# Two blocks behind each of three layer norms in fp32 from (x - shift) g, and lo of the expert tiles to VectorE at tile 41

## The chip, the cores and the metric

One core of one Trainium2 chip. The metric is device microseconds (us) of one execution; a kernel's time is the median of its runs. TensorE (PE) multiplies, VectorE (DVE) and ScalarE (ACT) work on tiles and read TensorE's results from PSUM, GpSimd (POOL) works on tiles in SBUF and issues gathers, and SyncE (SP) holds the queue that issues the other transfers.

## The reference

A two-layer encoder on 256 tokens (272 with 16 meta tokens in front), 1024 features. Layer 0 mixes tokens with a gated recurrence, layer 1 with a gated convolution of 31 taps; each is followed by a retrieval from 128 x 128 = 16384 experts, and behind each of the four sub-layers stands a layer norm:

```python
def layer_norm(x, g, b):
    mu = mean(x); var = mean(square(x - mu))
    return (x - mu) * rsqrt(var + LN_EPS) * g + b

def peer_block(xc, w_query, sub_keys, expert_u, expert_v):
    q = (xc @ w_query).reshape(c, HEADS, 2, HALF)
    scores = einsum('chpk,pnk->chpn', q, sub_keys)
    s1, i1 = top_k(scores[:, :, 0], 16)
    s2, i2 = top_k(scores[:, :, 1], 16)
    s, flat = top_k(s1[..., :, None] + s2[..., None, :], 16)
    g = softmax(s)
    act = gelu(expert_u[expert] . xc)
    return sum(g * act * expert_v[expert])

for i in range(2):
    h = layer_norm(ALPHA * h + mixer(h), ln_mix[i])
    h = layer_norm(ALPHA * h + peer(h), ln_ffn[i])
```

So a matrix product stands behind each of the first three norms: `w_query` of layer 0, `pw1` of the convolution, `w_query` of layer 1.

## The kernel before

Activations are kept with features on the 128 partitions, in eight blocks of 128 (NB), and tokens along the row (272 in layer 0, 256 in layer 1). A weight matrix is walked in output blocks of 128 columns, 512 KB each, loaded by SP into one of four raw buffers (`load`, L122 to L128).

Most products run in three parts of reduced fp32 (`linears`, L166): ScalarE rounds a raw block to `hi` (L137), the remainder `lo` is made by VectorE or GpSimd (L144), and TensorE makes 8 products each of `hi` by x's `hi`, `hi` by x's `lo`, and `lo` by x's `hi` (L172), in that order. `lo` has two buffers, so the `lo` of a block can be made one block ahead. The first two blocks (`defer=2`) are interleaved. `linears_whole` (L203, L208) instead multiplies a block in plain fp32, with 8 products; `w_in` and `pw1` go that way.

**The norms** (`normed`, L273). While the last blocks of the linear ahead of the norm come out, each finished block has the mean of all features, guessed from three blocks, taken away (`shift`), its square is made by ScalarE (`square`, L745) and summed by TensorE into `var`. Behind the last block TensorE sums the mean of what is left (`mu`) and the last square (L287), ScalarE squares the mean (L289), TensorE takes it from `var` (L290), and 13 products of ones follow whose result isn't used (`keep_clock`, L292). VectorE then subtracts `mu` from the eight blocks (L280), makes the reciprocal root with a Newton step (L310 to L312) and multiplies the eight blocks by it (L316). ScalarE and GpSimd apply gain and bias. Behind the first and the third norm (`norm_split`, L320) this gives x's `hi` at once (L324, L326), and VectorE makes x's `lo` (L331, L332). The query blocks' copies to q are VectorE's (L516).

**The convolution stage** (`conv_glu`, L1033). Blocks of `pw1` come in pairs, gate and value: ScalarE makes the sigmoid of the gate (L1045), VectorE multiplies (`hp`, L1051). ScalarE makes the first two taps of a block (L1074, L1076), VectorE the other 29 (L1078), for five blocks and most of a sixth; the rest goes through TensorE with diagonal matrices, which ScalarE makes (L1014).

**The expert stage** (`peer`, L496). Tokens are scored, and VectorE finds the top 16 of each head, in two token tiles of up to 128 (`topk_steps`, L777): 16 searches of the keys' scores, 8 of the sums, then copies of the indices and a one-hot product that reads the chosen indices out (L818, L821, L826). Meanwhile TensorE walks the 128 expert tiles U: 64 in the loop of L556, whose results `u_store` (L537) takes. There `lo` is made by GpSimd up to tile 45 and by VectorE from tile 46 (LO_FROM). Sixteen tokens are handled apart with gathered rows: from tile 40 (DOTS_FROM), at every second tile, GpSimd issues a gather (`few_rows`, L893) and, two steps later, VectorE makes a dot product (`few_dot`, L900), ten in all. From tile 54 the softmax of each token tile (L830) and the transposes of the chosen indices (`topk_out`, L959) follow. Behind tile 64 the one-hot weights of the experts are made (L577).

Instructions are ordered on each engine by a scheduler when the kernel is built; the order on an engine is then fixed. `issue_after(i)` puts what it holds behind i on i's engine. `pins` ties the rounding of the next weights to points of the norm.

Of the kernel before, what the change touches and what calls it, by code (L numbers as in the profile page):

```python
# [17 lines left out]
P = 128  # L18
# [17 lines left out]
DOTS_FROM, DOTS, AHEAD, LO_FROM = 40, 10, 2, 46  # L36
# [23 lines left out]
class Trunk:  # L60
    def __init__(self, tc, a):
        self.tc, self.nc, self.a = tc, tc.nc, a
        self.early = []
        self.squares = []
        self.last_diag = None
        self.turn = {}
        self.pins = []
        self.ahead = {}

# [140 lines left out]

    def split_x(self, src, hi, lo, hi_on="a"):
# [61 lines left out]
    def normed(self, sp, y, n, shifted=False):  # L273
# [8 lines left out]
        if shifted:  # L282
# [7 lines left out]
            self.mm = nc.tensor.matmul(var[:, :n], self.minus, sq[:, :n], start=False, stop=True)  # L290
            i, self.early_hi = self.early_hi, None
            self.keep_clock(13)  # L292
# [19 lines left out]
        nc.vector.scalar_tensor_tensor(r[1], r[1], 1.5, r[0], op0=OP.add, op1=OP.mult)  # L312
        for k in range(NB):
# [22 lines left out]
    def recurrent(self):  # L336
        tc, nc, a = self.tc, self.nc, self.a
        n = T0
        with tc.tile_pool(name="mix0", bufs=2) as sp:
# [7 lines left out]
            gw = sp.tile([P, 4, NB, P], F32, name="gw", bufs=1)  # L347
# [101 lines left out]

            self.linears([a["w_out"][b] for b in range(NB)], lambda k, lo: (hl if lo else hh)[:, k, :], n,  # L450
# [32 lines left out]
    def to_peer(self, sp, y, layer, n):  # L483
# [4 lines left out]
        def done(k):  # L488
            if k % 4 == 3:
# [3 lines left out]
                        lambda k: xs(k, 0)[:, :n], lambda k: xs(k, 1)[:, :n], done, True)  # L493
        return xs

    def peer(self, layer, n, xs):  # L496
# [10 lines left out]
        with tc.tile_pool(name=f"few{layer}", bufs=1) as kp:  # L507
# [5 lines left out]
            with tc.tile_pool(name=f"top{layer}", bufs=1) as sp:  # L513
                q = sp.tile([P, 2 * HEADS, nq], F32, name="q")
                self.linears([a["w_query"][layer, b] for b in range(2 * HEADS)], xs, nq, FULL,
                             lambda b, ps: nc.vector.tensor_copy(q[:, b, :], ps), defer=2,  # L516
# [3 lines left out]
                for c0, m in ctiles:  # L520
# [8 lines left out]
                    picked.append((c0, m, *self.topk(sp, sc, m)))  # L529
# [215 lines left out]
    def square(self, sp, y, i, n):  # L745
# [3 lines left out]
        sq = self.nc.scalar.activation(to, y[:, i, :n], AF.Square)  # L749
        if i == NB - 2:  # L750
# [26 lines left out]
    def topk_steps(self, sp, sc, m, H):  # L777
# [19 lines left out]
        for h in range(H):  # L797
# [19 lines left out]
        pairs = [m, 2 * H * K, K // 2, 2]  # L817
        nc.vector.tensor_tensor(oh[:m].rearrange("p g k (a b) -> p (g k) a b", b=2),  # L818
                                self.iota16[:m].rearrange("p (a b) -> p a b", b=2)[:, None].to_broadcast(pairs),
                                pf[:m, :, None, :].to_broadcast(pairs), op=OP.is_equal)  # L820
        nc.vector.tensor_tensor(oh[:m], oh[:m],  # L821
# [376 lines left out]
```

## Time and profile before

| | us |
|---|---|
| median of 3 runs | 1840.94 (1838.32 to 1842.51) |
| the profiled execution's own time | 1839.31 |
| its span | 1837.5 |
| TensorE busy | 1789.9 (97%) |
| VectorE busy | 1530.3 (83%) |
| ScalarE busy | 906.9 (49%) |
| GpSimd busy | 480.7 (26%) |

In the profile a time such as 117.33 is us from the start of the span. TensorE's busy time counts products from issue to modelled end, so it includes what they wait inside the engine. A plain fp32 product stands as two records. In a timeline a row gives start, length, engine, line, operation and shapes, how many were merged, and in brackets the idle time ahead of it with what ended it. The three norms of the change end near 117, 924 and 1053; the expert loops of 64 tiles begin near 181 and 1114. Each stage has its own limit, so a share of the whole span says little of any of them.

### The profile page before, as it was taken

The numbers are of one execution on the slowest core, as the hardware profiler recorded it, in microseconds if no ns is written. First come the engines' busy times: TensorE is split into PE (matmuls) and PEld (weight loads), VectorE is DVE, ScalarE is ACT, GpSimd is POOL, SyncE is SP. The second block draws the span as 40 slices with busy tenths as digits, with TensorE's granted clock in tenths as the row PEclk, the third lists the DMA queues.
The fourth block names the chain that finished last, engine by engine and source line by source line (L and its number), as shares of the span: only waits on it lengthen the run. The fifth ranks groups of instructions, "written<-read, shape, count | busy, mean of one in ns | idle before, by whom it ended". The sixth has DMA issues, their size and how long they took to land.

```text
span 1837.5 us, 35134 instructions
## 1 busy us (share of the span) xinstructions
PE 1789.9 (97%) x13599; PEld 1696.7 (92%) x13599; DVE 1530.3 (83%) x2812; ACT 906.9 (49%) x1478; POOL 480.7 (26%) x328
## 2 busy tenths in 40 slices
PE   8999998999999999999999999999999999999997
PEld 7889998999999999999878799999999999999996
DVE  7776997889998787777689859997889988868876
ACT  6544544554444544885432545445544444545542
POOL 1112998100001231222000017992000012423310
PEclk9999999999999999999999999999999999999998
DMA  5444566755557887988532365668555568989883
GB/s 196 138 164 159 169 193 220 244 182 165 162 168 250 308 318 268 321 276 279 176 115 79 106 192 157 191 195 286 180 167 171 164 237 316 333 298 336 294 279 127
DMA packets 110231, 394.10 MB, mean 214 GB/s; under 512 B 12144, under 2 KB 13296, under 8 KB 109936
## 3 DMA queue, kind: packets, MB, share of 16 engines
q1 hardware_dynamic: 91632, 324.74, 53.3%
q0 software_dynamic: 18432, 67.12, 10.5%
q8 instruction: 107, 1.75, 0.4%
q14 instruction: 60, 0.49, 0.1%
HBM read 386.50 MB, written 5.31 MB: 213 GB/s over the span
## 4 chain that ended last, share of the span: by engine, by line
PE 84%; DVE 10%; POOL 2%; issue 2%; ACT 1%; DMA 1%; POOLq 0%; SPq 0%; DVEq 0%; ACTq 0%
PE u L172 41%; PE acc L636 22%; PE acc L640 12%; PE u L208 3%; DVE cy L1078 2%; POOL lo L144 2%; DVE odd L1078 2%; DVE lo L144 1%; PE g L594 1%; PE g L595 1%; PE sps L526 1%; PE wide_ps L869 1%; DMA raw<-peer_v 1%; PE var L759 0%; DVE x L280 0%
## 5 line engine op out<-in xcount | busy, mean ns | idle before, releaser
L137 ACT ACTIVATE hi<-raw 128x1024 fp32r<-128x1024 f32 x560 | 592.5, 1059 | 637.2 <-PE u L172 227.2
L144 DVE TENSOR_TENSOR lo<-raw,hi 128x1024 fp32r<-128x1024 f32 x468 | 572.1, 1227 | 179.8 <-PE acc L640 65.8
L172 PE MATMUL u<-xs,hi 128*128 128x240 f32 (+3 forms) x4608 | 580.7, 278 | 3.6 <-ACT xs L326 3.5
L172 PEld LDWEIGHTS u<-xs,hi 128*128 128x128 f32 x4608 | 548.9, 191 | 5.1 <-ACT xs L326 4.5
L636 PE MATMUL acc<-w,hi 128*128 128x480 f32 (+1 forms) x1984 | 458.3, 373 | 1.9 <-DVE w L217 1.9
L636 PEld LDWEIGHTS acc<-w,hi 128*128 128x128 f32 x1984 | 354.4, 188 | 35.1 <-DVE w L217 2.3
L172 PE MATMUL u<-xs,lo 128*128 128x240 f32 (+3 forms) x2304 | 314.7, 277 | 12.7 <-POOL lo L144 11.8
L172 PEld LDWEIGHTS u<-xs,lo 128*128 128x128 f32 x2304 | 286.9, 191 | 15.0 <-POOL lo L144 13.3
L640 PEld LDWEIGHTS acc<-w,lo 128*128 128x128 f32 x2048 | 268.0, 190 | 15.0 <-DVE lo L144 4.3
L640 PE MATMUL acc<-w,lo 128*128 128x240 f32 (+1 forms) x2048 | 271.9, 274 | 2.4 <-DVE lo L144 2.3
L144 POOL TENSOR_TENSOR lo<-raw,hi 128x1024 fp32r<-128x1024 f32 x92 | 240.0, 2625 | 84.3 <-ACT hi L137 64.7
L895 POOL DMA_INDIRECT rows<-u_rows,ids x64 | 94.0, 1469 | 641.0 <-DVE sv L786 450.0
L895 POOL DMA_INDIRECT rows<-peer_v,ids x64 | 102.1, 1595 | 227.3 <-DVE few_out L930 118.3
L208 PE MATMUL u<-x,raw 128*128 128x272 f32 x512 | 121.1, 397 | 7.0 <-DMA x<-h 5.2
L208 PEld LDWEIGHTS u<-x,raw 128*128 128x128 f32 x512 | 98.1, 192 | 28.0 <-DMA raw<-w_in 5.2
L904 DVE SCALAR_TENSOR_TENSOR rows<-rows,wide 128x1024 f32<-128x1024 f32 x64 | 79.0, 1234 | 0.3 <-DMA rows<-u_rows,ids 0.3
L601 ACT ACTIVATE act_b<-g 128x368 f32<-128x368 f32 (+43 forms) x58 | 22.6, 390 | 113.4 <-DVE act_b L564 95.2
L930 DVE SCALAR_TENSOR_TENSOR few_out<-rows,act,few_out 128x1024 f32<-128x1024 f32 x60 | 76.7, 1279 | 1.2 <-DMA rows<-peer_v,ids 1.2
L577 DVE TENSOR_TENSOR AB<-iota,iT 128x2048 f16<-128x2048 f16 x58 | 70.5, 1219 | 0.1
L594 PE MATMUL g<-AB 128*128 128x128 f16 x464 | 58.6, 220 | 0.0
L595 PE MATMUL g<-Bl,AB 128*128 128x128 f16 x464 | 58.0, 219 | 0.0
L217 DVE TENSOR_TENSOR w<-act_b,w 128x960 fp32r<-128x960 f32 (+1 forms) x32 | 35.9, 1122 | 22.7 <-ACT w L214 22.7
(255 smaller groups left out, 1710.1 us busy)
## 6 DMA issues: line engine op xcount, KB each, us to landing
raw<-peer_u SPq DMA_DIRECT2D x256, 512.0 KB
raw<-peer_v SPq DMA_DIRECT2D x248, 512.0 KB
raw<-w_query SPq DMA_DIRECT2D x32, 512.0 KB
raw<-pw SPq DMA_DIRECT2D x24, 512.0 KB
raw<-w_in SPq DMA_DIRECT2D x16, 512.0 KB
raw<-w_out SPq DMA_DIRECT2D x8, 512.0 KB
wide<-wide SPq DMA_DIRECT2D x8, 512.0 KB
raw<-peer_v SPq DMA_DIRECT2D x16, 256.0 KB
```

The source lines that it names most:

```text
L137: self.act_hi = nc.scalar.activation(hi, raw, AF.Copy).ins
L144: i = e.tensor_tensor(lo[:, s], raw[:, s], hi[:, s].bitcast(F32), op=OP.subtract)
L172: self.mm = nc.tensor.matmul(ps[:, :n], l[:, k, :], xs(k, r)[:, :n], start=start, stop=stop)
L208: self.mm = self.nc.tensor.matmul(ps[:, :n], raw[:, k, :], x[:, k, :n], start=k == 0, stop=k == NB - 1)
L594: nc.tensor.matmul(ps[:, c, :], A, Bh, start=True, stop=False)
L595: nc.tensor.matmul(ps[:, c, :], A, Bl, start=False, stop=True)
L636: self.mm = nc.tensor.matmul(acc[b][:, :2 * n].rearrange("p (a t) -> p a t", a=2), hi, w[:, :, :n], start=j == 0, stop=j == NK - JG - 1, s ...
L640: self.mm = nc.tensor.matmul(main[b][:, :n], hi if p_ else lo, w[:, i, :n], start=False, stop=j == NK - 1 and not p_, skip_group_check=True)
L895: self.nc.gpsimd.indirect_dma_start(out=t, out_offset=None, in_=table, in_offset=bass.IndirectOffsetOnAxis(ap=few["ids"][:, i, k:k + 1], a ...
L904: self.nc.vector.scalar_tensor_tensor(t, t, 1.0, few["x"], op0=OP.mult, op1=OP.mult, accum_out=few["act"][:, i:i + 1])
L930: nc.vector.scalar_tensor_tensor(few["out"], t, w, few["out"], op0=OP.mult, op1=OP.add)
L1078: nc.vector.scalar_tensor_tensor(z, h, w, z, op0=OP.mult, op1=OP.add)
```

## The change

At each of the three norms the first two blocks of the product behind it are no longer made from the normed x. With d = x - shift, the normed row is ((d - mu) rstd) g + b, so a product with weights W is rstd (W(d g) - mu W g) + W b. ScalarE writes d g for each block as its square is made (`square`), two more columns hold -g and b (`pre_open`), and TensorE multiplies both weight blocks by these in plain fp32 (`pre_products`), in place of the 13 products of ones. The product that completes the variance stands behind the second of the eight pairs. ScalarE copies `mu` out of PSUM (`still`). `pre_take` then adds mu times the column of -g, multiplies by rstd, and hands over the column of b as the bias. The two weight blocks are loaded when `pre_open` stands in the program: ahead of `w_out`, ahead of the sums that collect layer 0's experts, and ahead of `pw2`.

In the expert loop, `lo` comes from VectorE from tile 41; the gathers and dots start at tile 48 and go at three of four tiles; the top-k of the second token tile is written out up to its 24 searches, and its other steps, with the one-hot work in two halves, follow one per tile from tile 41, each behind that tile's `lo`. The start of each softmax also stands behind the tile's `lo`.

```diff
-DOTS_FROM, DOTS, AHEAD, LO_FROM = 40, 10, 2, 46
+DOTS_FROM, DOTS, AHEAD, LO_FROM = 48, 10, 2, 41
...
+    def pre_open(self, sp, n, gain, bias, i, srcs, ws=None):
+        t = sp.tile([P, NB, T0 + 2], F32, tag="pre_x", name="pre_x", bufs=1)[:, :, :n + 2]
+        if ws is None:
+            ws = sp.tile([P, 2, NB, P], F32, tag="pre_w", name="pre_w", bufs=1)
+        for w, src in zip((ws[:, 0], ws[:, 1]), srcs):
+            self.nc.sync.dma_start(w.rearrange("p k n -> p (k n)"), src)
+        o = _OFF[gain] + i
+        self.nc.gpsimd.tensor_scalar(t[:, :, n], self.par[:, o:o + NB], -1.0, None, op0=OP.mult)
+        self.nc.gpsimd.tensor_copy(t[:, :, n + 1], self.par[:, _OFF[bias] + i:_OFF[bias] + i + NB])
+        self.pre = t, o, ws
+
+    def pre_products(self, sp, mu, spread):
+        t, _, ws = self.pre
+        n = t.shape[2]
+        units = [(self.bank(3 + i, "pre"), w) for i, w in enumerate((ws[:, 0], ws[:, 1]))]
+        for k in range(NB):
+            for ps, raw in units:
+                i = self.nc.tensor.matmul(ps[:, :n], raw[:, k, :], t[:, k, :], start=k == 0, stop=k == NB - 1)
+            if k == 1:
+                with self.tc.issue_after(i.ins):
+                    spread()
+        n -= 2
+        still = sp.tile([P, T0], F32, tag="still", name="still", bufs=1)[:, :n]
+        self.nc.scalar.activation(still, mu[:, :n], AF.Copy)
+        self.pre, self.pre_out = None, (still, n, [ps for ps, _ in units])
+
+    def pre_take(self, i, add=None):
+        nc = self.nc
+        mu, n, units = self.pre_out
+        ps = units[i]
+        cols = self.cp.tile([P, 2], F32, tag=f"pre_c{i}", name="pre_c", bufs=1)
+        nc.vector.tensor_copy(cols, ps[:, n:n + 2])
+        t = ps[:, :n]
+        nc.vector.scalar_tensor_tensor(t, mu, cols[:, 0:1], t, op0=OP.mult, op1=OP.add)
+        nc.vector.tensor_tensor(t, t, self.rstd, op=OP.mult)
+        if add is not None:
+            nc.vector.tensor_tensor(cols[:, 1:2], cols[:, 1:2], add, op=OP.add)
+        return t, cols[:, 1:2]
...
-            self.mm = nc.tensor.matmul(var[:, :n], self.minus, sq[:, :n], start=False, stop=True)
+            self.pre_products(sp, mu, lambda: nc.tensor.matmul(var[:, :n], self.minus, sq[:, :n], start=False, stop=True))
             i, self.early_hi = self.early_hi, None
-            self.keep_clock(13)
...
+            self.pre_open(sp, n, "ln_mix_g", "ln_mix_b", 0, a["w_query"][0, 0:2], pre_w)
             self.linears([a["w_out"][b] for b in range(NB)], lambda k, lo: (hl if lo else hh)[:, k, :], n,
...
+        self.pre_q = [self.pre_take(i) for i in range(2)]
         return xs
...
-                self.linears([a["w_query"][layer, b] for b in range(2 * HEADS)], xs, nq, FULL,
-                             lambda b, ps: nc.vector.tensor_copy(q[:, b, :], ps), defer=2,
+                for b, (t, bias) in enumerate(self.pre_q):
+                    nc.scalar.activation(q[:, b, :], t, AF.Identity, bias=bias)
+                self.linears([a["w_query"][layer, b] for b in range(2, 2 * HEADS)], xs, nq, FULL,
+                             lambda b, ps: nc.vector.tensor_copy(q[:, 2 + b, :], ps), defer=2,
...
-                    picked.append((c0, m, *self.topk(sp, sc, m)))
+                    if c0 + m < n:
+                        picked.append((c0, m, *self.topk(sp, sc, m)))
+                    else:
+                        slow = self.topk_steps(sp, sc, m, HEADS, 2)
+                        for _ in range(3 * HEADS):
+                            next(slow)
+                        picked.append((c0, m))
...
-                    k, odd = divmod(j - DOTS_FROM, 2)
-                    if early and 0 <= k < DOTS + AHEAD and not odd:
+                    if j >= LO_FROM and len(picked[-1]) == 2:
+                        with tc.issue_after(self.dve_lo.ins):
+                            try:
+                                next(slow)
+                            except StopIteration as end:
+                                picked[-1] += end.value
+                    k, step = divmod(3 * (j - DOTS_FROM), 4)
+                    if early and 0 <= k < DOTS + AHEAD and step < 3:
...
-                        with tc.issue_after(last.ins):
+                        with tc.issue_after(last.ins), tc.issue_after(self.dve_lo.ins):
                             picked[t] = c0, m, idx, self.softmax(sp, fv, m)
...
+        t, o, _ = self.pre
+        self.nc.scalar.activation(t[:, i, :n], y[:, i, :n], AF.Copy, scale=self.par[:, o + i:o + i + 1])
...
+        w = 2 * H // parts
+        for g in range(0, 2 * H, w):
...
+                                    pf[:m, g * K:(g + w) * K, None, :].to_broadcast(pairs), op=OP.is_equal)
+            yield
...
+            self.pre_open(sp, n, "ln_ffn_g", "ln_ffn_b", 0, (a["pw1"][NB], a["pw1"][0]))
             self.collect(sp, acc, x, n)
...
+            self.pre_open(sp, m, "ln_mix_g", "ln_mix_b", NB, a["w_query"][1, 0:2])
...
+        for i in range(2):
+            consume(i, *self.pre_take(i, self.col("conf_b_pw1", NB * (1 - i))))
+        self.linears_whole([a["pw1"][b + o] for b in range(1, NB) for o in (NB, 0)], x, n,
+                           lambda i, ps: consume(i + 2, ps), (0, 1, 2, 7, 6))
...
-            z2 = sp.tile([P, m], F32, tag="odd", name="odd", bufs=6)
+            z2 = sp.tile([P, m], F32, tag="odd", name="odd", bufs=4)
```

## Rows read from the trace of the kernel before

**Rows 1.** The chain of waits that ended last, by engine (page, part 4).

```profile
PE 84%; DVE 10%; POOL 2%; issue 2%; ACT 1%; DMA 1%; POOLq 0%; SPq 0%; DVEq 0%; ACTq 0%
```

**Rows 2.** Waits of TensorE: who waited for whom: us in total, times, longest.

```profile
PE u L172 <- POOL lo L144: 11.8, 8, 3.6
```

**Rows 3.** Timeline behind the first norm: start us, us, engine, line, operation, [idle before].

```profile
112.53 2.97 PE L226 MATMUL idle<-ones 128*128 128x512 f16 x13
...
117.33 0.40 PE L172 MATMUL u<-xs,hi 128*128 128x272 f32 x1 [1.83 <-ACT xs L326]
...
124.58 1.21 DVE L144 TENSOR_TENSOR lo<-raw,hi 128x1024 fp32r<-128x1024 f32 x1
...
126.98 1.16 PE L172 MATMUL u<-xs,lo 128*128 128x272 f32 x8
...
129.97 1.16 PE L172 MATMUL u<-xs,lo 128*128 128x272 f32 x8
```

**Rows 4.** Timeline behind the second norm, into the convolution stage.

```profile
918.77 0.40 ACT L289 ACTIVATE sq<-mu 128x272 f32<-128x272 f32 x1
...
919.20 2.87 DVE L280 TENSOR_TENSOR x<-x,mu 128x272 f32<-128x272 f32 x8 [0.96 <-ACT sq L289]
...
924.56 17.70 PE L208 MATMUL u<-x,raw 128*128 128x272 f32 x76 [1.75 <-ACT x L984]
...
927.35 1.28 ACT L1045 ACT_TABLE_LOAD   x1
...
929.00 0.49 ACT L1045 ACTIVATE sg<-u,par 128x272 f32<-128x272 f32 x1 [0.37 <-PE u L208]
...
929.39 1.85 ACT L1014 ACTIVATE diag<-ident,par 128x128 f32<-128x128 f32 x6
...
932.29 0.50 DVE L1051 SCALAR_TENSOR_TENSOR hp<-u,par,sg 128x272 f32<-128x272 f32 x1 [5.76 <-PE u L208]
```

**Rows 5.** Busy time by stretch: PE, PEld, DVE, ACT, POOL, PEclk, DMA share, GB/s.

```profile
940.00:960.00 20.00, 20.00 (x89) 16.56 (x88) 20.00 (x52) 4.46 (x9) 0.00 (x0) 1.00 0.44 143
```

**Rows 6.** Timeline behind the third norm.

```profile
1060.52 1.22 DVE L144 TENSOR_TENSOR lo<-raw,hi 128x1024 fp32r<-128x1024 f32 x1
...
1062.16 1.10 PE L172 MATMUL u<-xs,lo 128*128 128x256 f32 x8
```

**Rows 7.** Timeline of TensorE, layer 0: expert tiles 40, 46 and 47 begin.

```profile
291.07 1.96 PE L172 MATMUL u<-xs,hi 128*128 128x240 f32 x16
...
315.92 1.96 PE L172 MATMUL u<-xs,hi 128*128 128x240 f32 x16
...
318.61 1.95 PE L172 MATMUL u<-xs,hi 128*128 128x240 f32 x16
```

**Rows 8.** Timeline of TensorE, layer 1: expert tiles 40 and 46 begin.

```profile
1223.34 1.95 PE L172 MATMUL u<-xs,hi 128*128 128x224 f32 x16
...
1244.76 1.95 PE L172 MATMUL u<-xs,hi 128*128 128x224 f32 x16
```

**Rows 9.** Timeline of GpSimd, layer 0, tiles 41 to 43.

```profile
292.50 7.89 POOL L144 TENSOR_TENSOR lo<-raw,hi 128x1024 fp32r<-128x1024 f32 x2
...
300.54 4.05 POOL L895 DMA_INDIRECT rows<-u_rows,ids  x1
```

**Rows 10.** Timeline of VectorE, layer 0: last top-k search, sum of the one-hot step.

```profile
285.85 0.42 DVE L805 FIND_INDEX8 fi<-fv,r 112x8 uint32<-112x256 f32 x1
...
298.21 4.42 DVE L826 TENSOR_REDUCE idx<-oh 112x256 f32<-112x4096 f16 x1
```

**Rows 11.** Timeline, layer 0, tiles 54 to 64: VectorE, and a wait of TensorE.

```profile
336.15 1.22 DVE L904 SCALAR_TENSOR_TENSOR rows<-rows,wide 128x1024 f32<-128x1024 f32 x1
...
345.17 2.35 DVE L144 TENSOR_TENSOR lo<-raw,hi 128x1024 fp32r<-128x1024 f32 x2
...
351.28 2.35 DVE L144 TENSOR_TENSOR lo<-raw,hi 128x1024 fp32r<-128x1024 f32 x2
...
364.75 1.17 PE L172 MATMUL u<-xs,lo 128*128 128x240 f32 x8 [0.44 <-DVE lo L144]
```

More of the change, by code (lines that the diff above doesn't have):

```diff
@@ L68, in __init__ @@
         self.ahead = {}
+        self.pre = None
     def col(self, name, i):
@@ L312, in normed @@
         nc.vector.scalar_tensor_tensor(r[1], r[1], 1.5, r[0], op0=OP.add, op1=OP.mult)
+        self.rstd = r[1]
         for k in range(NB):
@@ L346, in recurrent @@
             self.early.append(self.load(a["w_in"][2]))
-            gw = sp.tile([P, 4, NB, P], F32, name="gw", bufs=1)
+            gw, pre_w = (sp.tile([P, 4, NB, P], F32, tag="gw", name="gw", bufs=1) for _ in range(2))
             lam = self.par[:, _OFF["lru_lambda"]:_OFF["lru_lambda"] + 2 * NB]
@@ L775, in topk, with topk_steps @@
                 return done.value
-    def topk_steps(self, sp, sc, m, H):
+    def topk_steps(self, sp, sc, m, H, parts=1):
         nc = self.nc
@@ L816, in topk_steps @@
         oh = sp.tile([P, 2 * H, K, K], F16, tag="cand", name="oh", bufs=1)
[L817 to L821, printed above, removed]
-                                s16[:m].rearrange("p a h k -> p (a h) k")[:, :, None, :].to_broadcast([m, 2 * H, K, K]),
-                                op=OP.mult)
-        yield
-        idx = sp.tile([P, 2, H, K], F32, tag=f"idx{H}", name="idx", bufs=2)
-        nc.vector.tensor_reduce(idx[:m].rearrange("p a h k -> p (a h) k"), oh[:m], op=OP.add, axis=AX.X)
-        yield
+        idx = sp.tile([P, 2, H, K], F32, tag=f"idx{H}", name="idx", bufs=2)
+        w = 2 * H // parts
+        pairs = [m, w * K, K // 2, 2]
+        for g in range(0, 2 * H, w):
+            nc.vector.tensor_tensor(oh[:m, g:g + w].rearrange("p g k (a b) -> p (g k) a b", b=2),
+                                    self.iota16[:m].rearrange("p (a b) -> p a b", b=2)[:, None].to_broadcast(pairs),
+                                    pf[:m, g * K:(g + w) * K, None, :].to_broadcast(pairs), op=OP.is_equal)
+            yield
+        for g in range(0, 2 * H, w):
+            s = s16[:m].rearrange("p a h k -> p (a h) k")[:, g:g + w, None, :]
+            nc.vector.tensor_tensor(oh[:m, g:g + w], oh[:m, g:g + w], s.to_broadcast([m, w, K, K]), op=OP.mult)
+            yield
+        for g in range(0, 2 * H, w):
+            nc.vector.tensor_reduce(idx[:m].rearrange("p a h k -> p (a h) k")[:, g:g + w], oh[:m, g:g + w],
+                                    op=OP.add, axis=AX.X)
+            yield
         return idx, fv
@@ L1039, in conv_glu, with consume @@
         state = {}
-        def consume(i, ps):
+        def consume(i, ps, bias=None):
             b = i // 2
@@ L1044, in consume @@
                 sg = sp.tile([P, n], F32, tag="sg", name="sg")
-                g = nc.scalar.activation(sg, ps, AF.Sigmoid, bias=self.col("conf_b_pw1", NB + b))
+                g = nc.scalar.activation(sg, ps, AF.Sigmoid, bias=self.col("conf_b_pw1", NB + b) if bias is None else bias)
                 state.setdefault("first", g)
@@ L1050, in consume @@
                 nc.gpsimd.memset(hp[:, n:n + HALO], 0.0)
-                nc.vector.scalar_tensor_tensor(hp[:, 0:n], ps, self.col("conf_b_pw1", b), state["sg"],
+                nc.vector.scalar_tensor_tensor(hp[:, 0:n], ps, self.col("conf_b_pw1", b) if bias is None else bias, state["sg"],
                                                op0=OP.add, op1=OP.mult)
@@ L1056, in consume @@
                     self.split_x(hp, *parts[b])
-        self.linears_whole([a["pw1"][b + o] for b in range(NB) for o in (NB, 0)], x, n, consume, (0, 1, 2, 7, 6))
+        for i in range(2):
+            consume(i, *self.pre_take(i, self.col("conf_b_pw1", NB * (1 - i))))
+        self.linears_whole([a["pw1"][b + o] for b in range(1, NB) for o in (NB, 0)], x, n,
+                           lambda i, ps: consume(i + 2, ps), (0, 1, 2, 7, 6))
         s = META - HALO
```

## The prediction

> **What bounds the kernel now.** I read the chain of waits first. TensorE holds 84% of it and VectorE 10% [rows 1], so the change is worth what it takes out of TensorE's queue, except in a stage where VectorE sets the end. Next the waits of TensorE: in the query and expert products it waited for a `lo` made on GpSimd eight times, 11.8 us in all, 3.6 us the longest [rows 2]. Then the timeline around the three norms. Behind the first, 13 idle products begin at 112.53 and the first query product comes only at 117.33 [rows 3]: a hole of 4.8 us, filled with work that computes nothing. The other two norms look alike. Behind the second lies the convolution, where VectorE is busy 20.00 of 20.00 us [rows 5], so that stage ends when VectorE ends, and what counts is when its first tap can start. Last, the expert stage: tile 40 of layer 0 begins at 291.07 and tile 46, the first whose `lo` is on VectorE, at 315.92, where six tiles at 2.69 would be 16.1 [rows 7]. GpSimd is the reason: two of its `lo` took 7.89 us and the gather behind them 4.05 [rows 9].
>
> **The norms: the products.** A block of eight fp32 products runs in 16 records, and 76 records took 17.70 us [rows 4], 0.23 each. So two blocks are 32 x 0.23 = 7.4 us, plus 0.5 for the variance product put between. They start where the idle products and the one ahead of them started, about 112.1 behind the first norm, and end at 120.0, 2.6 us after the old first query product [rows 3]. The variance itself stands behind four of the 16 products, 8 x 0.23 = 1.8 us late; I cost that at nothing, because the eight subtractions of the mean (2.87 us [rows 4]) cover it. Without that cover it is 1.8 us on the path in each norm.
>
> **The norms: what comes ahead of the subtractions.** The change adds two ScalarE operations at the end of each sum: (x - shift) g of the last block, ahead of the square of the mean, and the copy of the mean, behind it. That square took 0.40 us, and behind the second norm the subtractions start at 919.20, where it ends [rows 4], though they use nothing of it: both read the mean's bank. The copy reads that bank too, so I let the subtractions wait for both, 2 x 0.40 = 0.8 us a norm, between 0 (the scheduler puts the copy behind them) and 1.2. The Trainium skill's page "PSUM — Partial Sum Buffer", section "PSUM bank collisions raise a hardware error", says that two engines on one bank are kept apart, reads against reads too. By that rule the 0.8 us are due in full; by none of it they would be 0.4, for the copy of the last block alone; row 919.20 agrees with the rule.
>
> **First norm.** Two query blocks fewer are 2 x 2.99 = 5.99 us of TensorE, from one `lo` part to the next (126.98 to 129.97 [rows 3]). Against this: the first two blocks now run from 120.0 to 126.0. Before, the third block's `hi` part (two thirds of 2.99) began at 126.98 - 2.0 = 125.0. That is 1.0 late. VectorE, which made the third block's `lo` at 124.58 [rows 3], does so 0.8 later for the norm and behind the new reads of the two early blocks: four operations at 2.87 / 8 = 0.36 (the subtractions, same width) and two or more on two columns, between 0 and 0.36 each; 1.9 us for all. It ends at 124.58 + 0.8 + 1.9 + 1.2 = 128.5, where TensorE wants it at 128.0. Queued behind it on VectorE are the next `lo` and the copies of q, which have a bank ring of five to absorb them. So 1.5 us late, and 5.99 - 1.5 = 4.5 gained; 5.0 if the `lo` goes ahead of the reads, 3.5 if all bounds fall badly.
>
> **Third norm.** The blocks are 256 wide: 5.99 x 256 / 272 = 5.6. Here the third `lo` began at 1060.52 and the products that use it at 1062.16 [rows 6], a slack of only 0.4. With 0.8 and 1.9 more VectorE is 2.3 late: 3.3 gained, between 2.4 and 4.8.
>
> **Second norm.** Fewer blocks save TensorE time that the stage doesn't need. VectorE's first use, `hp`, came at 932.29 behind the sigmoid (929.00) and the second block [rows 4]. Now both blocks are there at 927.2. The multiplications end 0.8 late, ScalarE's table load ends at 927.35 + 0.8 + 1.28 = 929.4, the sigmoid at 929.9, `hp` follows: 2.4 earlier. But the 1.85 us of diagonals which ScalarE did while it waited [rows 4] now stand before the first two taps, which only ScalarE makes: then about 1.0 earlier. I take 1.5, between 0 and 2.4.
>
> The loads move too: SP's queue carries two weight blocks (512 KB each) ahead of `w_out`, ahead of the last expert tiles of layer 0 and ahead of `pw2`. They are the loads left out later, and each is asked for a whole product stage ahead of its use; I cost them at nothing, since the tiles held in the four raw buffers cover a late load; without that cover it is about the time of one tile, 2.7. The two GpSimd copies of eight columns per norm wait for nothing. Fewer "odd" buffers (four) cost nothing, as blocks come slower than VectorE's 31 taps finish. Norms together: 4.5 + 1.5 + 3.3 = 9.3, between 5.9 and 12.2.
>
> **The expert tiles.** Moving `lo` of tiles 41 to 45 to VectorE and the gathers behind tile 48 removes all of GpSimd's delay: 24.85 - 16.1 = 8.7 in layer 0; in layer 1 tiles 40 to 46 took 1244.76 - 1223.34 = 21.4 [rows 8], so 5.3. It is 14.0 in all if VectorE keeps up. First, is it free at tile 41? Its last top-k search ended at 285.85 [rows 10], and the copy of indices and the softmax start that stood in between move away; TensorE wants that `lo` near 295: yes, with 9 us to spare; layer 1 runs the same order. The moved steps, one behind each `lo`: the longest, the sum, is 4.42 us whole [rows 10], 2.2 in halves, plus 1.22 for the `lo`: 3.4 in a tile of 2.69, twice; VectorE falls 1.5 behind, which the tile of lead in the two `lo` buffers takes.
>
> The price comes later. Ten dot products (1.22 us, [rows 11]) went one in two tiles, from tile 44 on; they now go three in four, from 51. Tiles 54 to 63 get three more, 3.7 us, just where the softmax stands. There VectorE needs 351.28 - 345.17 = 6.1 us for two tiles, which are 5.4 of TensorE, and catches up with two `lo` back to back; TensorE already waited 0.44 for one of them at 364.75 [rows 11]. So between 0 (the idle time before tile 54 and the lead of one tile take it) and 3.7 a layer is given back. I take 2.0, nearer to the wait that is already there than to none. Expert tiles: 14.0 - 4.0 = 10.0, between 6.6 and 14.0.
>
> **Sum.** 9.3 + 10.0 = 19.3 us, between 12.5 and 26.2. The profiled execution took 1839.3 (span 1837.5 and 1.8 around it), 1.6 below the median of the three runs: 1820.0, and by the median 1821.6. About 0.2%, 3.7 us, is what a measurement of this kernel can tell from no change.
>
> **Rivals.**
> - *VectorE becomes the bound from tile 54.* For it: the 6.1 against 5.4. Against it: at 48 to 53 VectorE needs at most 1.22 + 1.22 of each 2.69, so it comes to tile 54 without a backlog. If the backlog costs 5 a layer, 4 is left of the 14.0: 13.3 gained, 1827.6.
> - *The norms' holes were covered anyway.* What follows each norm is set by VectorE (the splitting of x to 124.58, the taps), not by TensorE. For it: the 0.4 us of slack in the third norm. Against it: 14 blocks follow, and those are TensorE's alone. With the norms at 3: 13.0 gained, 1827.9.
> - *The variance doesn't come where the code puts it:* the scheduler lets all 16 products go first. Then it is 12 x 0.46 = 5.5 later, less 0.7 of cover, 4.8 in three norms: 5 gained, 1836. Against it: the order is pinned to the second pair.
> - *Slower: the gathers and VectorE get in each other's way.* Place: tiles 48 to 63, where GpSimd makes its gathers while VectorE has `lo`, dots and softmax without gaps. Price: the gather at 300.54 took 4.05 beside VectorE's sum [rows 9, 10]; if VectorE were held as long in turn, 12 x 4.05 = 49 us a layer. It decides from (14.0 + 9.3) / 2 = 11.7 a layer; at 15 the kernel takes 1847.6. Against it: at 298.21 VectorE's sum ran its 4.42 to the end and GpSimd waited. The Trainium skill's page "SBUF — State Buffer", section "SBUF: two separate sides", calls the port that the two share an exclusive lock for whoever starts first; by that the loss could fall on either, and the rows show it only on GpSimd's side.
>
> **How the numbers follow.** Forecast 0.66 (faster). VectorE the bound 0.14 and covered holes 0.10 (both faster). Variance late 0.06, half of it within 0.2%. Slower by the port 0.04. So faster 0.93, same 0.03, slower 0.04. The range reaches from near the best sum (26 gained and a little more, 1813.5) to 1830, past both of the nearer rivals; the last two cases lie beyond it, and the ends of the sum's bounds.
>
> **What would show it.** Right: no idle products behind the three norms, 32 fp32 records there, and query blocks 14 times; subtractions of the mean starting some 0.8 after the square; `hp` 1 to 2.4 earlier against the multiplications; no wait of TensorE for GpSimd between tiles 40 and 46 and full granted clock there; waits for VectorE's `lo` of a few us between tiles 54 and 64. Wrong: tiles 41 to 47 waiting for VectorE (its searches ended too late), or first query blocks that start more than 3 us after the old time, or a convolution stage that VectorE starts no earlier.

## The result, and the profile after

The kernel after takes 1819.99 us, median of 4 runs (1819.34 to 1821.12), against 1840.74 before (1838.32 to 1842.51): ratio 0.9885, 95% interval 0.9871 to 0.9899. The profiled execution spans 1817.7 us, 19.8 less than before. TensorE's waits, total us, times, longest:

```profile
PE mu L335 <- DVE total L825: 6.8, 1, 6.8
...
PE u L173 <- DVE lo L145: 3.0, 2, 1.9
PE u L173 <- POOL lo L145: 2.8, 2, 1.4
```

Of GpSimd's 11.8 us [rows 2] 2.8 are left, none at tiles 40 to 46. Two waits have grown: that for VectorE's `lo` from 0.9 us to 3.0, and that for the sum of the norm behind the convolution from 1.7 to 6.8. In the kernel before the latter was

```profile
PE mu L296 <- DVE total L767: 1.7, 1, 1.7
```

Behind the first norm the timeline now reads:

```profile
110.35 0.62 PE L229 MATMUL pre<-pre_x,gw 128*128 128x274 f32 x2
...
112.42 2.87 DVE L320 TENSOR_TENSOR x<-x,mu 128x272 f32<-128x272 f32 x8 [0.40 <-ACT still L235]
...
113.12 0.62 PE L330 MATMUL var<-sq,minus 128*128 128x272 f32 x2
113.57 5.71 PE L229 MATMUL pre<-pre_x,gw 128*128 128x274 f32 x24
...
118.92 0.49 PE L173 MATMUL u<-xs,hi 128*128 128x272 f32 x1
...
124.79 3.86 PE L173 MATMUL u<-xs,hi 128*128 128x272 f32 x28 [0.38 <-DVE xs L372]
...
126.71 1.22 DVE L145 TENSOR_TENSOR lo<-raw,hi 128x1024 fp32r<-128x1024 f32 x1
...
128.48 1.16 PE L173 MATMUL u<-xs,lo 128*128 128x272 f32 x8
...
129.48 1.66 PE L173 MATMUL u<-xs,hi 128*128 128x272 f32 x12
```

The fp32 products stand where the idle ones stood, and the first query product follows them without the wait of 1.83 in [rows 3]. The clock behind the norm differs too. In the kernel before, the busy time by stretch (the figure behind the five engines is the granted clock) reads

```profile
118.00:121.00 3.00, 3.00 (x16) 3.00 (x15) 3.00 (x8) 2.85 (x5) 2.79 (x4) 0.50 0.00 0
```

and in the kernel after the clock stays at 1.00 there. Of the expert tiles, 40 and 46 of layer 0, then of layer 1, begin at

```profile
285.61 1.96 PE L173 MATMUL u<-xs,hi 128*128 128x240 f32 x16
...
301.77 1.96 PE L173 MATMUL u<-xs,hi 128*128 128x240 f32 x16
...
1208.29 1.95 PE L173 MATMUL u<-xs,hi 128*128 128x224 f32 x16
...
1224.37 1.95 PE L173 MATMUL u<-xs,hi 128*128 128x224 f32 x16
```

16.16 and 16.08 us, where [rows 7, 8] give 24.85 and 21.42.

Single executions start up to 1.4 us apart, so I cut every trace into stages between starts of TensorE products: **A** first norm's sum to tile 0; **B** tiles 40 to 46 of layer 0 and **C** its tiles 46 to 66; **D** the shift product of the second norm to that of the third; **E** from there to tile 0 of layer 1; **F**, **G** its tiles 40 to 46 and 46 to 66. Us, each the difference of two start times:

| kernel | A | B | C | D | E | F | G |
|---|---|---|---|---|---|---|---|
| before | 70.14 | 24.85 | 56.10 | 122.75 | 84.82 | 21.42 | 55.04 |
| after | 64.97 | 16.16 | 57.70 | 123.97 | 80.33 | 16.08 | 55.84 |
| norms only | 65.01 | 23.30 | 56.09 | 125.27 | 80.32 | 21.37 | 55.37 |
| tiles only | 70.56 | 16.16 | 57.53 | 122.74 | 84.82 | 16.08 | 56.51 |
| second norm as before | 64.95 | 16.14 | 56.90 | 122.82 | 80.33 | 16.08 | 56.46 |
| eight dots | 65.02 | 16.16 | 62.73 | 124.03 | 80.36 | 16.09 | 59.83 |
| masks behind lo | 64.97 | 16.16 | 55.62 | 123.84 | 80.46 | 16.08 | 54.89 |
| clock kept | 64.97 | 16.14 | 57.87 | 122.62 | 80.48 | 16.08 | 55.85 |
| variance last | 68.98 | 16.14 | 56.90 | 128.92 | 83.97 | 16.08 | 58.57 |
| copy behind | 64.95 | 16.14 | 57.35 | 124.44 | 80.45 | 16.08 | 55.85 |
| lo from 46 | 65.01 | 16.16 | 58.30 | 124.46 | 80.54 | 16.08 | 60.36 |
| three repairs | 64.96 | 16.14 | 57.23 | 121.18 | 80.46 | 16.08 | 54.48 |
| masks, no second | 64.97 | 16.16 | 55.59 | 122.80 | 80.33 | 16.08 | 54.47 |
| repairs, eight dots | 64.96 | 16.14 | 55.53 | 121.13 | 80.32 | 16.08 | 54.47 |

The gains are in A (5.17), B (8.69), E (4.49) and F (5.34); C, D and G give back 1.60, 1.22 and 0.80. The sum at which A starts itself comes 0.26 later behind the shift than before, since two of the early products stand ahead of it; counted from the shift, the first norm gives 4.91. Beyond the stages, the last one (tile 66 of layer 1 to the end) takes 537.0 to 540.7 us from one trace to the next with no system that follows the edits. I take that for the noise behind the medians.

### The profile page after: what moved, and what is told of

The parts are those of the page before. It is cut to its first block, busy times and chain, and to the rows that moved or that the text cites. A ratio compares the mean times of both kernels' runs of the same rounds, so it can differ in the third digit from the quotient of the medians.

```text
span 1817.7 us, 35024 instructions
## 1 busy us (share of the span) xinstructions
PE 1777.5 (98%) x13528; PEld 1689.8 (93%) x13528; DVE 1517.3 (83%) x2840; ACT 912.8 (50%) x1505; POOL 445.6 (25%) x324
## 4 chain that ended last, share of the span: by engine, by line
PE 69%; DVE 8%; DMA 2%; issue 1%; ACT 1%; POOL 0%; POOLq 0%; DVEq 0%; ACTq 0%; SPq 0%
PE u L173 30%; PE acc L692 21%; PE acc L696 12%; DVE cy L1146 2%; DVE odd L1146 2%; PE g L650 1%; PE g L651 1%; DVE lo L145 1%; DMA raw<-peer_v 1%; DMA rows<-u_rows,ids 0%; PE pre L229 0%; PE sps L570 0%; POOL lo L145 0%; PE acc L731 0%; PE var L817 0%
## 5 line engine op out<-in xcount | busy, mean ns | idle before, releaser
L145 DVE TENSOR_TENSOR lo<-raw,hi 128x1024 fp32r<-128x1024 f32 x474 | 578.2, 1223 | 179.8 <-PE acc L696 68.3
L173 PE MATMUL u<-xs,hi 128*128 128x224 f32 (+3 forms) x4544 | 568.4, 276 | 0.6 <-DVE xs L372 0.6
L173 PEld LDWEIGHTS u<-xs,hi 128*128 128x128 f32 x4544 | 536.9, 190 | 1.4 <-DVE xs L372 1.2
L173 PE MATMUL u<-xs,lo 128*128 128x224 f32 (+3 forms) x2272 | 307.0, 276 | 5.8 <-DVE lo L145 3.0
L173 PEld LDWEIGHTS u<-xs,lo 128*128 128x128 f32 x2272 | 280.4, 190 | 7.2 <-DVE lo L145 3.4
L958 POOL DMA_INDIRECT rows<-u_rows,ids x64 | 86.7, 1355 | 667.8 <-DVE sv L844 429.3
L145 POOL TENSOR_TENSOR lo<-raw,hi 128x1024 fp32r<-128x1024 f32 x82 | 210.5, 2582 | 73.1 <-ACT hi L138 55.4
L209 PE MATMUL u<-x,raw 128*128 128x272 f32 x480 | 113.9, 397 | 5.3 <-DMA x<-h 5.3
L209 PEld LDWEIGHTS u<-x,raw 128*128 128x128 f32 x480 | 92.4, 193 | 24.6 <-DMA raw<-w_in 5.2
```

The costliest lines, as they stand in the source:

```text
L145: i = e.tensor_tensor(lo[:, s], raw[:, s], hi[:, s].bitcast(F32), op=OP.subtract)
L173: self.mm = nc.tensor.matmul(ps[:, :n], l[:, k, :], xs(k, r)[:, :n], start=start, stop=stop)
L209: self.mm = self.nc.tensor.matmul(ps[:, :n], raw[:, k, :], x[:, k, :n], start=k == 0, stop=k == NB - 1)
L958: self.nc.gpsimd.indirect_dma_start(out=t, out_offset=None, in_=table, in_offset=bass.IndirectOffsetOnAxis(ap=few["ids"][:, i, k:k + 1], a ...
```

## The experiments

**Each half alone.** The first kernel keeps the expert tiles of before, the second the norms of before:

```diff
-DOTS_FROM, DOTS, AHEAD, LO_FROM = 48, 10, 2, 41
+DOTS_FROM, DOTS, AHEAD, LO_FROM = 40, 10, 2, 46
...
-                    if j >= LO_FROM and len(picked[-1]) == 2:
...
-            self.pre_products(sp, mu, ...)
+            self.mm = nc.tensor.matmul(var[:, :n], self.minus, sq[:, :n], start=False, stop=True)
+            self.keep_clock(13)
```

> The kernel after, with the expert tiles as in the kernel before (lo of U on VectorE from tile 46, gathers and dots from tile 40 in every second tile, the one-hot steps whole and ahead of the product loop). Theory from the two traces: the norms are worth 5.0 behind the first norm, 0.2 behind the second, 4.6 behind the third, less 1.4 in the stage of pw2, so 8.4 in all and a ratio to before of 0.9954 (1832.3 against 1840.7), between 7.4 and 9.4. Forecast: 9.3. Rival (covered holes: part of what stands at tile 0 of the expert loop is lost again at tiles 40 to 46, where GpSimd sets the time): under 6, ratio over 0.9967.

> The kernel after, with the three norms as in the kernel before (idle products, all query and pw1 blocks in their loops). Theory from the two traces: 8.7 and 5.3 gained at tiles 40 to 46, 0.3 at tile 32, less the waits for lo at tile 64 (2.1 and some 0.5 to 1) and 0.8 lost at the end of layer 0: 11.4 in all, ratio 0.9938 (1829.3), between 10.4 and 12.4. Forecast: 10.0. Were the two parts to lean on each other, e1 and e2 would not add up to the 20.7 of both.

Measured: 1833.38 (ratio 0.9960, 0.9946 to 0.9973) and 1830.45 (0.9947, 0.9934 to 0.9961). By these the norms give 7.2 and the tiles 10.1, 17.3 together where both give 20.7; each is below the range that its theory gave. In the table the halves add up: A and E come whole with the norms, B and F with the tiles (1.55 of B comes with the norms alone too; stage D, 125.27 in the first, belongs to the next two experiments). In these two traces the last stage, which neither edit touches, is longer (539.2 and 540.7, 537.5 after); I don't put that down to the change. Whether it is also what the medians lack isn't shown. "Covered holes" falls: A and E are not given back at the tiles.

**The second norm taken back.** Its two blocks return to the loop and the idle products come back:

```diff
-            self.pre_open(sp, n, "ln_ffn_g", "ln_ffn_b", 0, (a["pw1"][NB], a["pw1"][0]))
...
-            consume(i, *self.pre_take(i, self.col("conf_b_pw1", NB * (1 - i))))
-        self.linears_whole([a["pw1"][b + o] for b in range(1, NB) for o in (NB, 0)], x, n,
+        self.linears_whole([a["pw1"][b + o] for b in range(NB) for o in (NB, 0)], x, n, consume, (0, 1, 2, 7, 6))
```

> The kernel after, but behind the second norm as in the kernel before (idle products, all 16 blocks of pw1 in the loop, no scaled copies there). Theory from the two traces: VectorE's first tap came only 0.2 earlier against the shift, so the time is that of the kernel after, within 0.7 (1819.3 to 1820.7). Forecast: the second norm gave 1.5, so 1821.5.

Measured: 1820.89 (0.9897, 0.9882 to 0.9913), which doesn't tell 0 from 1.5. The trace does: stage D is 122.82, as before, against 123.97. So this part did not gain, it cost 1.2 in these two traces. Where, the timeline of TensorE after shows:

```profile
984.73 6.48 PE L1156 MATMUL cv<-hs,diag 128*128 128x256 f32 x53
991.05 1.04 PE L266 MATMUL idle<-ones 128*128 128x512 f16 x4
998.93 1.22 PE L335 MATMUL mu<-total,ones 128*128 128x256 f32 x2 [6.84 <-DVE total L825]
999.94 1.91 PE L266 MATMUL idle<-ones 128*128 128x512 f16 x4
1001.65 3.99 PE L341 MATMUL var<-sq,ones 128*128 128x256 f32 x16
...
1009.30 0.39 PE L173 MATMUL u<-ch,hi 128*128 128x256 f32 x1 [1.50 <-DVE ch L1065]
```

and the busy time by stretch:

```profile
990.00:995.00 5.00, 2.09 (x15) 1.31 (x13) 5.00 (x13) 0.47 (x1) 0.00 (x0) 1.00 0.00 0
995.00:1000.00 5.00, 1.07 (x3) 0.70 (x4) 3.88 (x10) 0.00 (x0) 0.00 (x0) 0.56 0.34 105
1000.00:1005.00 5.00, 5.00 (x19) 3.67 (x18) 2.73 (x8) 3.71 (x9) 0.00 (x0) 0.76 0.00 0
```

VectorE sets the end of the convolution, and TensorE, with fewer blocks, is done earlier and stands for 6.84 us. The clock falls to 0.56, near its lower level (1.2 of 2.4 GHz). The sum then takes 1.22 instead of 0.70, four idle products 1.91 instead of 1.03. From that sum to the first product of `pw2` it is 10.37 us; before, the same way took 9.04 behind a wait of 1.69.

**The clock kept.**

```diff
-            self.keep_clock(4)
+            self.keep_clock(28)
             self.mm = nc.tensor.matmul(mu[:, :n], self.ones, self.total, start=True, stop=True)
```

> The kernel after, with 28 instead of 4 idle products ahead of the sum of the norm behind the convolution, where TensorE now waits 6.84 us. Theory: in that wait the granted clock falls to 0.56, and the sum, the idle products and the squares behind it run at it, 10.4 us from that sum to the first product of pw2 where it was 9.0 before; with the idle products the 9.0 come back, 1.3 us, 1818.7. Rival: the 1.3 us come from something else in that stage (ScalarE's load, the tiles called odd), and the 10.4 stay.

Measured: 1818.93 (0.9882, 0.9866 to 0.9897). In the timeline of TensorE:

```profile
990.05 6.22 PE L266 MATMUL idle<-ones 128*128 128x512 f16 x28
997.95 0.70 PE L335 MATMUL mu<-total,ones 128*128 128x256 f32 x2 [1.68 <-DVE total L825]
...
1006.98 0.39 PE L173 MATMUL u<-ch,hi 128*128 128x256 f32 x1 [1.50 <-DVE ch L1065]
```

9.03 us, and D falls by 1.35 to 122.62. The loss was the clock. All the traces agree: from the sum of that norm to the third shift it takes 18.17 to 18.25 us in the seven kernels where TensorE waits 0.2 to 1.7 for that sum, and 19.30 to 20.62 in the seven where it waits 6.6 to 7.0. So the pause costs 1.1 to 2.4 us, and the 125.27 of the norms alone is its upper end. The Trainium skill's page "TensorE: Matmul & The Clock Gate", section "HAM oscillation — how this bites in real kernels", says that pauses in TensorE's work send its clock back to half rate; these rows agree, with 0.56 behind a pause of 6.84 and 1.00 behind one of 1.68. The length of a pause doesn't tell by itself: in the kernel before, the wait of 1.83 behind the first norm was followed by 0.50 (above), and those of 1.75 and 1.7 behind the other two norms, with the same idle products ahead of them, by 1.00.

**Fewer dots.** This was to show that the new wait for `lo` is the backlog of the dots:

```diff
-DOTS_FROM, DOTS, AHEAD, LO_FROM = 48, 10, 2, 41
+DOTS_FROM, DOTS, AHEAD, LO_FROM = 48, 8, 2, 41
```

> The kernel after, with 8 instead of 10 dots of the early tile in the U products of each layer (the last at tile 61 and not 63; the other two a layer are made later, among the V products). Theory: the wait for lo at tile 64 is the backlog of VectorE behind the dots, so it goes: 2.1 and 1.4 gained, 1816.5, up to 1818.5 if part of it moves. Rival: the softmax and the first AB masks hold that lo whatever the dots do: 1819.5 to 1820. The trace must show it at tile 64.

Measured: 1830.24 (0.9946, 0.9932 to 0.9960), 10 us slower than after with less work on VectorE there. Both theories missed. The wait in the kernel after, at tile 64 (VectorE and TensorE):

```profile
350.03 2.36 DVE L633 TENSOR_TENSOR AB<-iota,iT 128x2048 f16<-128x2048 f16 x2
...
352.30 0.68 DVE L640 TENSOR_TENSOR Bl<-AB,glT 128x1024 f16<-128x1024 f16 x1
...
353.02 0.69 DVE L641 TENSOR_TENSOR AB<-AB,ghT 128x1024 f16<-128x1024 f16 x1
353.63 2.35 DVE L145 TENSOR_TENSOR lo<-raw,hi 128x1024 fp32r<-128x1024 f32 x2
354.90 1.17 PE L173 MATMUL u<-xs,lo 128*128 128x240 f32 x8 [1.87 <-DVE lo L145]
```

and with eight dots, where it comes three tiles earlier:

```profile
345.36 2.36 DVE L633 TENSOR_TENSOR AB<-iota,iT 128x2048 f16<-128x2048 f16 x2
...
348.96 2.35 DVE L145 TENSOR_TENSOR lo<-raw,hi 128x1024 fp32r<-128x1024 f32 x2
350.23 2.06 PE L173 MATMUL u<-xs,lo 128*128 128x240 f32 x8 [3.56 <-DVE lo L145]
...
352.10 3.62 PE L173 MATMUL u<-xs,hi 128*128 128x240 f32 x16
```

In both, the one-hot masks `AB` of the gate products, 3.6 us with what belongs to them, are put on VectorE as soon as the dots are through, ahead of two `lo` that are wanted first. With eight dots they come sooner, the wait is 3.56, and the products behind it run at half the clock: 16 in 3.62 us instead of 1.96.

```profile
350.00:355.00 5.00, 4.77 (x22) 4.77 (x23) 2.54 (x3) 1.43 (x2) 0.00 (x0) 0.50 0.66 205
```

In the kernel after the wait of 1.87 left the clock at 1.00.

**The masks pinned.**

```diff
+                    with tc.issue_after(self.dve_lo.ins):
-                    nc.vector.tensor_tensor(AB.rearrange(...), keys, ..., op=OP.is_equal)
+                        nc.vector.tensor_tensor(AB.rearrange(...), keys, ..., op=OP.is_equal)
```

> The kernel after, with the one-hot masks AB of the gate products pinned behind the lo of their own tile, and nothing else. Theory, from the kernel with eight dots: what holds back the lo at tile 64 are the masks, 3.7 us of VectorE that are put ahead of two lo as soon as the dots are done, so the wait of 1.87 (layer 0) and 1.12 (layer 1) goes, tiles 54 to 66 of layer 0 take 34.1 to 34.6 instead of 36.15, and the kernel 2 to 3 us less: 1817 to 1818. Rival (the forecast's reason): the backlog is that of the dots, so the wait stays or moves to a tile nearby and the time is 1819 to 1821.

Measured: 1816.34 (0.9875, 0.9859 to 0.9890). Now one `lo` stands ahead of the first mask, and no wait is left:

```profile
351.69 1.23 DVE L145 TENSOR_TENSOR lo<-raw,hi 128x1024 fp32r<-128x1024 f32 x1 [1.00 <-PE u L173]
352.83 1.22 DVE L634 TENSOR_TENSOR AB<-iota,iT 128x2048 f16<-128x2048 f16 x1
...
355.42 1.22 DVE L145 TENSOR_TENSOR lo<-raw,hi 128x1024 fp32r<-128x1024 f32 x1
...
355.91 1.06 PE L173 MATMUL u<-xs,lo 128*128 128x240 f32 x8
```

C and G fall by 2.08 and 0.95, below what they were before the change. (In the six kernels with these tiles and free masks C lies between 56.90 and 57.87, so 1.3 of the fall in C is clear of that spread.)

**The variance last.** The third rival, made true:

```diff
-            if k == 1:
+            if k == NB - 1:
```

> The kernel after, with the variance product of each norm behind all 16 products of the two early blocks instead of behind four of them. Prices the third rival of the forecast, which said 4.8 a norm: 1834. From the trace of the kernel after: the subtractions end at 115.29 and the variance would come at 119.8, so 4.5 a norm, 13.5 in all, 1833.5, between 1831 and 1835 if the second norm's stage takes some of it. Rival: other work covers it (the reads of the early blocks go first, the two blocks are done anyway), under 6 in all, below 1826.

Measured: 1833.10 (0.9963, 0.9949 to 0.9977). A, D and E grow by 4.01, 4.95 and 3.64. Behind the first norm:

```profile
118.94 0.62 PE L330 MATMUL var<-sq,minus 128*128 128x272 f32 x2
...
122.69 0.59 PE L173 MATMUL u<-xs,hi 128*128 128x272 f32 x1 [3.13 <-ACT xs L366]
```

So the place of that one product is worth more than half of the whole change. Part of it is clock again: in the 5 us from 120, behind the wait of 3.13, it was 0.74. (G is 2.73 longer than after in this trace, with a wait of 1.7 for a `lo` and one of 1.6 for a `z`; the edit doesn't touch these.)

**The copy of the mean behind the subtractions.**

```diff
-        self.nc.scalar.activation(still, mu[:, :n], AF.Copy)
+        self.still = lambda: self.nc.scalar.activation(still, mu[:, :n], AF.Copy)
...
             for k in range(NB):
                 center(k)
+            with self.tc.issue_after(self.last_center.ins):
+                self.still()
```

> The kernel after, with the copy of the mean put behind the subtractions of the mean instead of ahead of them. Theory (two engines don't read one bank at a time, so the subtractions wait for the copy): they start 0.4 earlier against the sum in each norm, and the time falls by 0.4 to 1.2, to 1819 or 1819.5. Rival: they wait for the square of the mean alone or for the sum, and start where they did; or the copy now holds the scaled copies of ScalarE up by the same 0.4, and the time stays at 1820.

Measured: 1820.09 (0.9894, 0.9877 to 0.9910). Behind the first norm the mean's product begins at 110.81 after and at 111.10 here, and the subtractions at 112.42 in both:

```profile
112.01 0.38 ACT L329 ACTIVATE sq<-mu 128x272 f32<-128x272 f32 x1
...
112.42 2.87 DVE L320 TENSOR_TENSOR x<-x,mu 128x272 f32<-128x272 f32 x8
```

They start 0.29 earlier against the sum, so they had waited for the copy. Now they start where the square of the mean ends (112.01 + 0.38), the other read of that bank by ScalarE; the `lo` ahead of them on VectorE had ended at 112.30. That agrees with the Trainium skill's page "PSUM — Partial Sum Buffer", section "PSUM bank collisions raise a hardware error", by which two engines' reads of a bank are kept apart too. Stages A and E don't move (64.95, 80.45): TensorE comes to its first query product from the 32 early records, not from the norm, and later still waits for x's `lo`, 0.43 here and 0.38 after.

**Lo from tile 46.** One constant, so GpSimd makes `lo` up to tile 45, while the gathers and the one-hot steps stay behind that:

```diff
-DOTS_FROM, DOTS, AHEAD, LO_FROM = 48, 10, 2, 41
+DOTS_FROM, DOTS, AHEAD, LO_FROM = 48, 10, 2, 46
```

> The kernel after, with lo of U on VectorE from tile 46 only, as in the kernel before, while the gathers, the dots and the one-hot steps stay behind it (one-hot steps one a tile from tile 46). Tells which part of the change freed GpSimd at tiles 40 to 46. Theory A (the gathers and the one-hot steps made GpSimd late, moving its lo away was not needed): tiles 40 to 46 take 16.2 in layer 0 and 16.1 in layer 1 as in the kernel after, and the time stays within 1.5 of 1820. Theory B (its lo is too slow by itself): 18 or more, up to the 23 to 25 of the kernel before, and 1823 to 1830.

Measured: 1826.71 (0.9927, 0.9913 to 0.9940). Theory A holds at the tiles (B 16.16, F 16.08) and misses the time. GpSimd keeps up:

```profile
289.69 2.39 POOL L145 TENSOR_TENSOR lo<-raw,hi 128x1024 fp32r<-128x1024 f32 x1 [0.30 <-PE u L173]
```

Two of these took 7.89 in [rows 9], beside the one-hot steps of VectorE. But now these steps come from tile 46 on and push the softmax: in layer 1 TensorE waits for its `z`, and G grows to 60.36.

```profile
1259.76 0.33 PE L1027 MATMUL tps<-ident,z 128*128 128x128 f32 x1 [3.08 <-DVE z L908]
```

So the time falls where theory B had it, for a reason that neither theory named.

**Repairs together.** The pinned masks, the kept clock, and the diagonals of block 5 behind ScalarE's first two taps:

```diff
-        with tc.issue_after(state["first"].ins):
-            for b in CONV_ORDER:
-                for k in on_pe[b] if b not in SPLIT else ():
-                    self.diagonal(sp, 0, b, k, self.par[:, _OFF["conf_dw_w"]:])
...
                     i = nc.scalar.activation(z, h, AF.Copy, scale=w)
+                    if b == 0:
+                        with tc.issue_after(i.ins):
...
```

> The kernel after with three repairs: the masks pinned behind lo (as in the kernel so named), the 28 idle products ahead of the norm behind the convolution (as in the kernel with the clock kept), and the six diagonals of block 5 behind the first two taps of block 0 on ScalarE instead of ahead of them. Theory: the diagonals hold the first tap on VectorE by 1.5 to 1.9 us, VectorE sets the end of that stage, so from the shift of the second norm to the shift of the third it takes 120.7 to 121.1 (122.75 before, 123.97 after, 122.62 with the clock kept), and the kernel 1813.5, between 1812.5 and 1815. Rival: the first tap waits for hp or the sigmoid anyway, 122.6 stays, 1815 to 1816.

Measured: 1816.17 (0.9871, 0.9856 to 0.9886), above the range of both. D is 121.18, as the theory said, 1.44 below the clock alone. In the kernel after the first tap on VectorE stood behind the diagonals:

```profile
916.89 1.28 ACT L1110 ACT_TABLE_LOAD   x1 [0.75 <-DVE pre L246]
...
918.71 0.50 DVE L1116 SCALAR_TENSOR_TENSOR hp<-pre,pre_c,sg 128x272 f32<-128x272 f32 x1 [1.49 <-ACT sg L1110]
...
919.14 1.85 ACT L1079 ACTIVATE diag<-ident,par 128x128 f32<-128x128 f32 x6
920.89 0.59 ACT L1142 ACTIVATE cy<-hp,par 128x256 f32<-128x256 f32 x1
...
921.51 0.48 DVE L1146 SCALAR_TENSOR_TENSOR cy<-hp,par,cy 128x256 f32<-128x256 f32 x1 [2.30 <-ACT cy L1142]
```

Repaired it comes 1.17 behind `hp` instead of 2.80:

```profile
918.25 0.50 DVE L1117 SCALAR_TENSOR_TENSOR hp<-pre,pre_c,sg 128x272 f32<-128x272 f32 x1 [1.49 <-ACT sg L1111]
...
919.42 0.48 DVE L1148 SCALAR_TENSOR_TENSOR cy<-hp,par,cy 128x256 f32<-128x256 f32 x1 [0.67 <-ACT cy L1139]
```

What kept the sum from 1813.5 is C (57.23 against 55.62): in this execution a transpose waited 1.17 for the softmax's `z`.

> The kernel after with the masks pinned behind lo, and the second norm as in the kernel before. Theory: the second norm's part of the change costs 1.2 us as it stands (122.8 instead of 124.0 between the two shifts), so 1815.2 where the pinned masks alone gave 1816.3. Rival (the forecast): that part gains 1.5, so 1817.8.

The edits are those of the kernel with the masks pinned and of the one with the second norm taken back. Measured: 1817.78 (0.9880, 0.9865 to 0.9895), the rival's number, while D, 122.80 against 123.84, says the theory's. Here and with the second norm taken back alone, the medians say the opposite of stage D, by 1.4 and 0.9, within their spread. So what the second norm's part costs is shown for that stage only; the whole kernel's time doesn't tell.

> The kernel with the three repairs, with 8 instead of 10 dots of the early tile in each layer's U products, as in the kernel with eight dots that took 1830. Theory: that kernel lost its time to the masks alone, which were put 1.5 tiles earlier once the dots were gone; with the masks pinned no wait for lo over 0.5 is left at tiles 54 to 66, those take 33.8 to 34.6, the granted clock stays at 1.00 there, and the time is 1814 to 1817. Rival (fewer dots cost by themselves, by what moves to the V products or by another step that comes forward): 1820 or more.

Measured: 1814.59 (0.9856, 0.9834 to 0.9878), the fastest of all. TensorE waits nowhere in tiles 54 to 66 of layer 0, C is 55.53 and the clock 1.00. So the 10 us of the eight dots were due to the masks alone, with the clock that fell behind the wait for them.

## Why the prediction was right, and where not

Forecast 1821.6, measured 1820.0; the sum was 19.3 and came to 19.8. That it came so close is partly luck: the second norm fell 2.7 short, and the first (0.4 more, from the shift), the third (1.2 more) and the backlog (1.6 less in both layers) made up for it. Step by step:

- **First norm**, forecast 4.5, measured 5.17 in A, 4.91 from the shift. The `lo` products of the third block in the loop begin at 128.48, 1.50 later than in [rows 3]. That is the figure worked out, but not for its reason: VectorE's `lo` for them is ready at 127.93 and TensorE doesn't wait for it. TensorE comes from its early products sooner than forecast (first query product at 118.92), then waits 0.38 for x's `lo`, which the forecast had at nothing, and does four products of the loop's fourth block first (12 follow at 129.48 and not 16). These four, 0.5 us, are why it is 6.5 shorter from there to tile 0 and not 5.99. The 0.8 for the bank came to 0.4 to 0.6 a norm against the shift, 0.27 to 0.29 of it the copy; putting the copy behind moved neither A nor E. And the forecast overlooked the clock: before, 15 products behind the norm ran at 0.50, in 3.4 us where the next 15 take 1.9. So up to 1.5 us of this gain may be clock; no run separates it.
- **Third norm**, forecast 3.3, measured 4.49 in E. I let VectorE's third `lo` be 2.3 late and TensorE wait for it. TensorE doesn't wait for that `lo`, only 0.24 for x's.
- **Second norm**, forecast 1.5, at worst 0; measured 1.22 lost in D. This step failed, in the sentence "Fewer blocks save TensorE time that the stage doesn't need". Of the way from the shift product to `hp`, 1.8 was gained (25.97 us before, 24.16 after) and not 2.4, as ScalarE's table load stood behind VectorE's reads of the early blocks, which I had left out of this norm; but to the first tap on VectorE only 0.2: the diagonals took 1.6, not the 1.4 worked out. And the time that the stage doesn't need became a pause of TensorE, which cost 1.3 of clock behind it (1.1 to 2.4 over the traces). With both mended D is 1.6 below before, about the 1.5 I had claimed.
- **Expert tiles**, forecast 8.7 and 5.3, measured 8.69 and 5.34. The number was right, and its reason half: the one-hot steps and gathers had to go from tiles 41 to 45, the `lo` did not. What its move buys, as I read that run, is a place for these steps ahead of the softmax; a kernel with the steps at tile 41 and `lo` on GpSimd was not run. GpSimd's `lo` took 3.95 beside them (half of 7.89, [rows 9]) and 2.39 without. The Trainium skill's page "SBUF — State Buffer", section "SBUF: two separate sides", has the two engines share one port pair that whoever starts first keeps; these rows agree, with the loss on GpSimd. It falls on VectorE too, in kernels that let GpSimd's `lo` run late: with the norms alone a dot of layer 1 took 5.59 us and not 1.2, and in the kernel before one took 2.23.

```profile
1227.32 4.71 POOL L145 TENSOR_TENSOR lo<-raw,hi 128x1024 fp32r<-128x1024 f32 x2
1227.53 5.59 DVE L950 SCALAR_TENSOR_TENSOR rows<-rows,wide 128x1024 f32<-128x1024 f32 x1
```

- **Backlog**, forecast 2.0 a layer, measured 1.60 and 0.80 in C and G. The size lay within its bounds, the cause was wrong: not the dots, but the masks that follow them.
- **Loads**, at nothing. From tile 66 of layer 0 to the second norm's shift it is 534.3 us before, 535.1 after, 534.3 with the norms alone and 534.8 with the tiles alone: no loss that follows the loads.
- **Rivals.** VectorE as the bound would have cost 5 a layer. The late variance, forecast 4.8 a norm, was priced at 4.01, 4.95 and 3.64. The price of the port on VectorE's side did not appear at tiles 48 to 63: its dots beside the gathers take 1.21 to 1.23 us, as in [rows 11]. Beside GpSimd's `lo` there is one, as shown above, and the change keeps the two apart.

## What to carry to other kernels

Work taken off TensorE in a stage that another engine ends becomes a pause, and a pause can be paid for at the clock of what follows; fill it, or move work into it. A wait for an engine's product is read from what stands directly ahead of it in that engine's order, not from how busy it is: two dots fewer made the kernel 10 us slower, masks pinned behind one `lo` 3.6 us faster. And before an operation is moved away from a slow engine, look at what ran beside it.

## What the runs showed that was not expected

A wait of 3.56 us of TensorE was followed by a stretch at clock 0.50, one of 1.87 by none, and yet one of 1.83, in the kernel before, by 0.50. A dot on VectorE took 5.59 us beside two `lo` of GpSimd, and 1.2 beside gathers. Moving a single product of 0.5 us by 24 records cost 4.2 us a norm, on average of the three, waits and clock included.
